# Attention by pairs of heads: scores as three 64-row matmuls in two row halves

## The chip, the cores and the metric

The kernel runs on one core of a Trainium2 chip. The time is the device time of one execution in microseconds; the median of three runs is given. Engines are named as in the profile: PE is TensorE (matmul), PEld its weight load, DVE is VectorE, ACT is ScalarE, POOL is GpSimd, SP is the engine whose queue issues the DMAs. L12 is line 12 of the kernel.

## The reference

One layer of a decoder trunk on 2048 positions of 1024 channels: a projection of the normalised input feeds three groups (an mLSTM of 4 heads, forgetting attention of 8 heads of 64, a spatial gating unit); their outputs go through `w_out`, then follows a convolutional FFN. The change concerns the attention:

```python
F = jnp.cumsum(jax.nn.log_sigmoid(f_pre), axis=-1)
for blk in range(s_len // Q_BLOCK):                  # blocks of 128 queries
    lo, hi = blk * Q_BLOCK, (blk + 1) * Q_BLOCK
    logits = (jnp.einsum('bhtd,bhsd->bhts', q[:, :, lo:hi], k[:, :, :hi]) * scale
              + F[:, :, lo:hi, None] - F[:, :, None, :hi])
    logits = jnp.where(mask, logits, -jnp.inf)       # causal
    p = jax.nn.softmax(logits, axis=-1)
    outs.append(jnp.einsum('bhts,bhsd->bhtd', p, v[:, :, :hi]))
```

q and k are RMS-normalised per head first. All is float32; the kernel's large matmuls run on float32r and split each operand in a rounded part (hi) and a remainder (lo), so that a product takes several matmuls.

## The kernel before

The stages in order of time: a projection by blocks of 256 columns of `w_in` (with the mLSTM in the background), attention, the `w_out` product, the FFN up and down. Tiles come from pools with tags; each tag has a fixed number of buffers, and a tile waits for the last user of its buffer. A scheduler orders the instructions of each engine when the program is built, so that steps of neighbouring loops stand between each other; the source gives the dependences and a priority.

*Projection of q and k* (`use_qk`, `turn`). For each of 16 row tiles of 128 positions and each group of four heads, L639 scales the projected columns by the norm and writes each head twice side by side (`[P, 4, 2, 64]`), four transposes (L648) turn it, ACT writes the hi part (L653 for q, L659 for k) and DVE the lo part (L655, L660). q goes to DRAM as two tensors, `qh_d` and `ql_d`, each with a head's 64 channels twice on 128 partitions; k as one, `kk_d`, with hi on partitions 0 to 63 and lo on 64 to 127.

*Scores* (`scores(h, tb)`), for head `h` and block `tb` of 512 queries. For each of four row blocks of 128 queries the keys up to the diagonal are walked in pieces of 512. A piece takes a PSUM tile `sp` (four buffers of 2 KB a partition) and two matmuls on all 128 rows, hi q by [k hi; k lo] (L190) and lo q by the same (L191), which gives all four products; on the last piece a bfloat16 matmul adds the causal mask (L193). One DVE operation adds the forget bias and takes the row maximum of the piece (L198, which comes with a read of the accumulator). Then follow the maximum over pieces (L203), the exponential with its sum on ACT (L206, pieces of 1024), the reciprocal of the sum (L209 to L212) and the scaling on POOL (L214).

*Values* (`finish(h, tb)`). For each of the 4 to 16 key blocks `j`, up to four transposes of 128x128 (L227) go to PSUM tile `tp` (three buffers), ACT takes the hi part (L230), DVE the lo part (L231), and two matmuls (L232, L233) add to `op` (one buffer). V holds hi and lo side by side, so that partitions 0 to 63 and 64 to 127 of `op` are summed at the end (L235, L236) and stored.

The loop runs over 8 heads and 4 blocks, `scores` and then `finish` of the same block. K, the bias row and V of a head are loaded whole (`load_head`). The last head takes the blocks in the order 2, 3, 0, 1, in which `w_out` uses them. The first half of `w_out` is loaded and split (`load_w`, L130, L131) after block 2 of head 6.

*Elsewhere 64-row matmuls occur* in the mLSTM (`mlstm`, L804 and L806), where two heads lie on the two halves of the partitions:

```python
for par in range(2):
    hp = slice(par * 64, par * 64 + 64)
    eo = mps()
    for j in range(2):
        T.matmul(eo[:, j * P : (j + 1) * P], kT[hp, j, :], qT[hp, j, ch], start=True, stop=True)
    for j in range(2):
        T.matmul(eo[:, 256 + j * 65 : 321 + j * 65], qT[hp, j, ch], Cst[hp, j, :], start=True, stop=True)
```

These operands are float32, for which the trace has two matmuls for each.

## Time and profile before

| | |
|---|---|
| median of three runs | 2768.22 us (2767.72 to 2775.49) |
| profiled execution | 2769.87 us, span 2768.2 us, granted clock 0.978 |
| PE busy | 2638.0 us, 95% |
| PEld busy | 2247.4 us, 81% |
| DVE busy | 2089.8 us, 75% |
| ACT busy | 1314.6 us, 47% |
| POOL busy | 374.6 us, 14% |

The span runs from the first to the last instruction. A group row reads: line, engine, operation, output<-inputs, shapes, count, busy us, mean ns of one, idle time of the engine before them and what ended it. [...] A timeline row reads: start, us, engine, line, operation, tiles, shape, count; a shape `64*128` says that 64 rows and 128 columns of the array are used.

### The profile page before, as it was taken

How to read it: one execution, taken by the hardware profiler on the slowest of the kernel's cores; microseconds unless marked ns; L12 is line 12 of the kernel's file. 1: busy time of each engine (PE TensorE's matmuls, PEld its weight loads, DVE VectorE, ACT ScalarE, POOL GpSimd, SP SyncE). 2: the span in 40 equal slices, each digit the busy share in tenths (PEclk: the TensorE clock that was granted, in tenths of full speed). 3: DMA queues.
4: the chain of work that ended last, by engine and by line, in shares of the span. 5: the costliest groups of instructions: out<-in, count | busy, mean ns of one | idle time of the engine just before them, and what ended most of it. 6: DMA issues, size and time to landing. Idle time of an engine off the chain costs nothing.

```text
span 2768.2 us, 40628 instructions
## 1 busy us (share of the span) xinstructions
PE 2638.0 (95%) x14473; PEld 2247.4 (81%) x14473; DVE 2089.8 (75%) x4090; ACT 1314.6 (47%) x2448; POOL 374.6 (14%) x400
## 2 busy tenths in 40 slices
PE   5989899989899999999998999999999999999999
PEld 5989888989797877767886888888788888888787
DVE  7366477246448999997567988887888887899797
ACT  4243244233226788776444544444444444444443
POOL 2032221032223334342000000000000000000000
PEclk9989999999899999999999999999999999999999
DMA  7534375324446234323663222227322223848533
GB/s 247 175 93 144 112 229 176 108 48 134 111 145 197 79 108 132 106 79 130 218 242 91 93 76 84 84 76 281 99 84 78 82 84 141 303 146 297 185 106 115
DMA packets 322561, 382.11 MB, mean 138 GB/s; under 512 B 28189, under 2 KB 227833, under 8 KB 320309
## 3 DMA queue, kind: packets, MB, share of 16 engines
q1 hardware_dynamic: 322356, 379.51, 42.3%
q8 instruction: 114, 1.87, 0.3%
q14 instruction: 91, 0.74, 0.1%
HBM read 274.47 MB, written 104.96 MB: 137 GB/s over the span
## 4 chain that ended last, share of the span: by engine, by line
PE 61%; DVE 5%; ACT 2%; issue 1%; DMA 1%; POOL 0%; DVEq 0%; ACTq 0%; POOLq 0%
PE ub L54 10%; PE ub L55 10%; PE ub L56 10%; PE db L55 4%; PE db L56 4%; PE db L54 4%; PE tp L227 4%; PE op L232 2%; PE op L233 2%; PE wps L56 2%; PE wps L54 2%; PE wps L55 2%; PE sp L190 2%; PE sp L191 1%; ACT L L206 1%
## 5 line engine op out<-in xcount | busy, mean ns | idle before, releaser
L54 PE MATMUL acc<-whi,hh 128*128 128x256 f32 (+1 forms) x1408 | 423.0, 301 | 23.8 <-DVE qn L639 10.5
L56 PE MATMUL acc<-whi,hl 128*128 128x256 f32 (+1 forms) x1408 | 411.1, 293 | 0.9 <-DVE hl L487 0.9
L55 PE MATMUL acc<-wlo,hh 128*128 128x256 f32 (+1 forms) x1408 | 411.3, 293 | 0.0
L54 PEld LDWEIGHTS acc<-whi,hh 128*128 128x128 f32 x1408 | 281.9, 200 | 30.9 <-DVE vhl L625 5.4
L55 PEld LDWEIGHTS acc<-wlo,hh 128*128 128x128 f32 x1408 | 282.3, 201 | 0.5 <-issue 0.2
L56 PEld LDWEIGHTS acc<-whi,hl 128*128 128x128 f32 x1408 | 281.3, 200 | 1.6 <-DVE hl L487 1.4
L54 PE MATMUL ub<-T,wsph 128*128 128x512 f32 x704 | 276.2, 393 | 5.8 <-ACT wsph L1150 5.8
L55 PE MATMUL ub<-T,wsph 128*128 128x512 f32 x704 | 276.0, 392 | 0.0
L56 PE MATMUL ub<-T,wspl 128*128 128x512 f32 x704 | 274.9, 391 | 0.4 <-DVE wspl L1151 0.4
L55 PE MATMUL db<-wspl,wsph 128*128 128x512 f32 x616 | 240.3, 390 | 1.9 <-DVE wspl L1282 1.9
L56 PE MATMUL db<-wsph,wspl 128*128 128x512 f32 x616 | 239.6, 389 | 0.0
L54 PE MATMUL db<-wsph 128*128 128x512 f32 x616 | 238.2, 389 | 0.3 <-ACT wsph L1281 0.3
L1150 ACT CAST wsph<-S 128x512 fp32r<-128x512 f32 x176 | 109.4, 621 | 231.4 <-PE ub L55 166.6
L56 PE MATMUL ub<-B,wspl 128*128 128x512 f32 x528 | 208.2, 394 | 2.1 <-DVE wspl L1151 2.1
L54 PE MATMUL ub<-B,wsph 128*128 128x512 f32 x528 | 208.4, 395 | 1.5 <-ACT wsph L1150 1.5
L55 PE MATMUL ub<-B,wsph 128*128 128x512 f32 x528 | 208.0, 394 | 0.0
L214 POOL TENSOR_SCALAR L<-L,ri 128x1024 f32<-128x1024 f32 (+2 forms) x192 | 168.3, 890 | 260.5 <-DVE nm L203 69.5
L206 ACT ACTIVATE L<-L,nm 128x1024 f32<-128x1024 f32 (+2 forms) x192 | 173.2, 903 | 55.7 <-DVE nm L203 54.5
L231 DVE TENSOR_TENSOR plo<-tp,phi 128x512 fp32r<-128x512 f32 (+1 forms) x320 | 186.8, 607 | 16.9 <-ACT phi L230 11.2
L198 DVE CUSTOM_DVE_ANT_0 L<-sp,nfb 128x512 f32<-128x512 f32 (+2 forms) x320 | 185.4, 601 | 5.5 <-PE sp L191 1.9
L227 PE MATMUL tp<-ident,L 128*128 128x128 f32 x1088 | 178.4, 276 | 6.1 <-POOL L L214 2.9
L230 ACT CAST phi<-tp 128x512 fp32r<-128x512 f32 (+1 forms) x320 | 157.7, 519 | 32.1 <-PE tp L227 28.3
(336 smaller groups left out, 6040.5 us busy)
## 6 DMA issues: line engine op xcount, KB each, us to landing
w<-in_w_up_dram SPq DMA_DIRECT2D x88, 512.0 KB
wd<-in_w_down_dram SPq DMA_DIRECT2D x176, 256.0 KB
wa<-in_w_ada_dram SPq DMA_DIRECT2D x96, 256.0 KB
wst<-in_w_in_dram SPq DMA_DIRECT2D x48, 512.0 KB
act_d<-yc SPq DMA_DIRECT2D x44, 512.0 KB
act<-act_d SPq DMA_DIRECT2D x44, 512.0 KB
hc_d<-hl SPq DMA_DIRECT2D x28, 512.0 KB
xt<-in_x_dram SPq DMA_DIRECT2D x16, 512.0 KB
```

Of the source, the lines that this page charges most:

```text
L54: T.matmul(ps, lh, rh, start=start, stop=False, skip_group_check=resume)
L55: T.matmul(ps, lh, rl, start=False, stop=False, skip_group_check=resume)
L56: T.matmul(ps, ll, rh, start=False, stop=stop, skip_group_check=resume)
L190: T.matmul(sp[:, :w], q2[0][:, qs], kk[:, s0 : s0 + w], start=True, stop=False)
L198: V.tensor_tensor_reduce(out=parts[-1][0][:, o : o + w], in0=sp[:, :w], in1=nf[:, s0 : s0 + w], scale=1.0, scalar=-3.0e38, op0=ALU.add, op ...
L206: A.activation(L[:, :w], L[:, :w], AF.Exp, bias=nm, accum_out=rs[:, j : j + 1])
L214: G.tensor_scalar(L[:, :w], L[:, :w], ri, 1.0, op0=ALU.mult, op1=ALU.mult)
L227: T.transpose(tp[:, i * P : (i + 1) * P], rows[i][j // 8][:, (j % 8) * P : (j % 8 + 1) * P], ident)
L230: A.copy(hi[:, c0:], tp[:, c0:])
L231: V.tensor_tensor(lo[:, c0:], tp[:, c0:], hi[:, c0:].bitcast(F32), op=ALU.subtract)
L232: T.matmul(op[:, c0:], vv[:, j, :], hi[:, c0:], start=(j == 0), stop=False)
L1150: A.copy(hi, src)
```

## The change

Heads are taken in four pairs. Head `2p` has partitions 0 to 63 and head `2p + 1` partitions 64 to 127 of every q and k tile.

- In the projection, `turn` no longer doubles a head's channels: L639's successor writes 256 columns for 512, two transposes for four turn a tile, and q and k each are stored as a hi and a lo tensor (`q_d`, `k_d`) of half the former size per tensor.
- `scores(p, tb)` is a generator. It walks the keys in chunks of up to 1024 for both heads at once, each head with its own PSUM tile `sp` (two buffers of 4 KB a partition). The mask is added first. Each 512 columns take three matmuls a head on its 64 rows (hi hi, hi lo, lo hi), written so that the two heads alternate. The DVE operation covers the chunk, keeps a running minimum of the negated logits across chunks (its start value is the first chunk's), and a separate maximum is not taken. The sum of two chunks is on POOL for both heads at once, one reciprocal serves both heads. Exponentials of the second head, reciprocal and scaling of a row block are held back behind the next DVE operations (`after`).
- `finish(p, tb, rows)` is a generator over both heads; its value products stand two steps behind the transposes (`behind`). `tp` and `op` have two buffers each.
- `phase(now, then)` steps the scores of block `now` and the values of the block before, `then`, in turn.
- The first block (pair 0, block 1) is written between the steps of the last projection block (`background`, `tick`).
- K and bias are loaded a pair ahead, V in four chunks; `w_out`'s first half is loaded at the last block of pair 3.

```diff
-    qh_d = dr.tile([NH, P, S], F32, name="qh_d")
-    ql_d = dr.tile([NH, P, S], F32, name="ql_d")
-    kk_d = dr.tile([NH, P, S], F32, name="kk_d")
+    q_d = dr.tile([NH // 2, 2, P, S], F32, name="q_d")
+    k_d = dr.tile([NH // 2, 2, P, S], F32, name="k_d")
...
-        pp.open("att_r", "right", ("sp", 2048, 4))
+        pp.open("att_r", "right", ("sp", 4096, 2))
...
-        pp.open("att_l", "left", ("tp", 2048, 3), ("op", 2048, 1))
+        pp.open("att_l", "left", ("tp", 2048, 2), ("op", 2048, 2))
...
+    def scores(p, tb, q2, rows):
+        kh, kl, nf = kv["k", p]
+        qh, ql = q2
+        after = []
         for i in range(4):
             n_s = (tb * 4 + i + 1) * P
-            npc = (n_s + 511) // 512
+            parts = [(s0, min(1024, n_s - s0)) for s0 in range(0, n_s, 1024)]
...
-                sp = pp.tile([P, 512], F32, name="sp")
-                last = j == npc - 1
-                T.matmul(sp[:, :w], q2[0][:, qs], kk[:, s0 : s0 + w], start=True, stop=False)
-                T.matmul(sp[:, :w], q2[1][:, qs], kk[:, s0 : s0 + w], start=False, stop=not last)
+                sp = [pp.tile([P, 1024], F32, name="sp", tag="sp") for _ in range(2)]
+                last = c == len(parts) - 1
                 if last:
-                    T.matmul(sp[:, w - P : w], identb, maskb, start=False, stop=True)
+                    for e in range(2):
+                        T.matmul(sp[e][:, w - P : w], identb, maskb, start=True, stop=False, skip_group_check=True)
+                for b in range(0, w, 512):
+                    bw = min(512, w - b)
+                    for n, (q_, k_) in enumerate(((qh, kh), (qh, kl), (ql, kh))):
+                        for e in range(2):
+                            hp = slice(e * 64, e * 64 + 64)
+                            T.matmul(
+                                sp[e][:, b : b + bw], q_[hp, qs], k_[hp, s0 + b : s0 + b + bw],
+                                start=n == 0 and not (last and b + bw == w), stop=n == 2, skip_group_check=True,
+                            )
+                for e in range(2):
+                    L[e, c] = pool.tile([P, w], F32, name="L", tag=l_tag(p, tb, i, e, c))
+                    V.tensor_tensor_reduce(
+                        out=L[e, c], in0=sp[e][:, :w], in1=nf[:, e, s0 : s0 + w], scale=-1.0,
+                        scalar=3.0e38 if c == 0 else nm[:, 2 * e : 2 * e + 1], op0=ALU.add, op1=ALU.min,
+                        accum_out=nm[:, 2 * e + c : 2 * e + c + 1],
+                    )
+                    if after:
+                        after.pop(0)()
+                    yield
...
+            def second(exps=exps, rs=rs, rr=rr, n=len(parts)):
+                exps(1)
+                if n == 2:
+                    G.tensor_tensor(rs[:, 0:2], rs[:, 0:2], rs[:, 2:4], op=ALU.add)
+
+            def third(L=L, rs=rs, rr=rr, n=len(parts)):
+                V.reciprocal(rr, rs[:, 0:2])
+                for e in range(2):
+                    for c in range(n):
+                        G.tensor_scalar(L[e, c], L[e, c], rr[:, e : e + 1], 1.0, op0=ALU.mult, op1=ALU.mult)
+
+            exps(0)
+            after += [second, third]
...
+        for e in range(2):
+            op = pp.tile([P, 512], F32, name="op", tag="op")
+            for j in range(ns):
...
+                behind.append((e, j, c0, hi, lo, op))
+                if len(behind) > 2:
+                    product(*behind.pop(0))
+                yield
...
+    def phase(now, then):
...
+        for n in range(n_sc):
+            next(sc)
+            while done < (n + 1) * (n_fin - 6) // n_sc:
+                next(fin)
+                done += 1
...
-            n = pool.tile([P, 4, 2, 64], F32, name="qn", tag="q2k")
+            n = pool.tile([P, 4, 64], F32, name="qn", tag="q2k")
...
-            for j in range(4):
-                T.transpose(tp[:, j * P : (j + 1) * P], n[:, j].rearrange("p e d -> p (e d)"), ident)
+            for j in range(2):
+                T.transpose(tp[:, j * P : (j + 1) * P], n[:, 2 * j : 2 * j + 2].rearrange("p e d -> p (e d)"), ident)
...
+    for p in range(4):
+        for n, tb in enumerate((1, 2, 3, 0) if p < 3 else TBS):
+            if n == 0:
+                if p < 3:
+                    load_k(p + 1)
+                load_v(p, 0)
+                load_v(p, 1)
+            if (p, n) == (3, 3):
+                pool.close("att_r")
+                wout_open_right()
                 load_w(0)
+            last = phase((p, tb), last) if (p, n) != (0, 0) else (0, 1, first_rows)
```

## The prediction

> **What bounds the kernel now.** I read the page's engine shares, then busy time by stretch to find the stage that the change touches, then the groups by line there, then the timeline for what one instruction really occupies.

> ```profile
> span 2768.2 us, 40628 instructions
> PE 2638.0 (95%) x14473; PEld 2247.4 (81%) x14473; DVE 2089.8 (75%) x4090; ACT 1314.6 (47%) x2448; POOL 374.6 (14%) x400
> 830.00:1290.00 460.00, 443.29 (x2614) 347.33 (x2613) 421.56 (x1344) 354.06 (x763) 177.45 (x200) 0.99 0.37 112
> 880.00:1200.00 320.00, 313.04 (x1878) 248.84 (x1876) 302.00 (x980) 257.02 (x561) 130.70 (x148) 1.00 0.36 111
> 947.60:1158.10 210.50, 206.77 (x1249) 165.38 (x1249) 198.97 (x660) 168.62 (x371) 83.15 (x98) 1.00 0.35 112
> ```

> In the stretches the columns are PE, PEld, DVE, ACT and POOL busy time, granted clock, DMA share and GB/s. Attention is 830 to 1290 us, the other stages hold no changed loop but the projection's q and k blocks. 947.6 to 1158.1 is four heads: 52.6 us a head, TensorE idle for 0.9 of them and VectorE for 2.9. Both are near full; ACT (42 a head) and DMA (0.35) are not.

> A busy PE is not a PE at its peak, so I take what a matmul occupies from start to start:

> ```profile
> 860.25 0.40 PE L191 MATMUL sp<-kk,q 128*128 128x512 f32 x1
> 860.48 0.39 PE L190 MATMUL sp<-kk,q 128*128 128x512 f32 x1
> 860.71 0.39 PE L233 MATMUL op<-plo,vv 128*128 128x512 f32 x1
> 861.75 0.92 PE L227 MATMUL tp<-ident,L 128*128 128x128 f32 x7
> ...
> 865.12 0.23 PE L193 MATMUL sp<-maskb,identb 128*128 128x128 bf16 x1
> ...
> 865.16 0.47 PE L190 MATMUL sp<-kk,q 128*128 128x512 f32 x1
> ```

> 512 columns cost 0.23 us; a transpose (0.92 - 0.27)/6 = 0.109, a mask 0.04. Per head the causal blocks are 136 squares of 128: 17,408 columns. Two score matmuls over them are 68 x 0.23 = 15.6 us, two value matmuls the same, 136 transposes 14.8, masks under 1: 46.7 of the 52.6. The other 5.9 a head (47 for eight) is idleness and weight loads that stand open after a wait.

> **The scores on TensorE.** Before, one head's hi and lo halves fill all 128 rows: 2 matmuls a piece, 640 in all, 278,528 columns, 544 x 0.23 = 125 us. After, 3 matmuls a piece on 64 rows for each head of a pair: 960, 417,792 columns. They gain only where the two row halves run side by side. The kernel already has 64-row matmuls, in the mLSTM part:

> ```profile
> 772.10 0.28 PE L55 MATMUL acc<-wlo,hh 128*128 128x256 f32 x1
> 772.22 0.28 PE L56 MATMUL acc<-whi,hl 128*128 128x256 f32 x1
> 772.43 0.71 PE L804 MATMUL mps<-qT,kT 64*128 64x128 f32 x4
> 772.98 0.22 PE L806 MATMUL mps<-Cst,qT 64*128 64x65 f32 x1
> 772.98 0.37 PE L804 MATMUL mps<-qT,kT 64*128 64x128 f32 x1
> 773.03 0.38 PE L806 MATMUL mps<-Cst,qT 64*128 64x65 f32 x2
> 773.20 0.27 PE L804 MATMUL mps<-qT,kT 64*128 64x128 f32 x1
> 773.26 0.27 PE L806 MATMUL mps<-Cst,qT 64*128 64x65 f32 x1
> 773.31 0.38 PE L804 MATMUL mps<-qT,kT 64*128 64x128 f32 x2
> 773.53 0.55 PE L806 MATMUL mps<-Cst,qT 64*128 64x65 f32 x4
> 774.01 0.44 PE L648 MATMUL trp<-ident,qn 128*128 128x128 f32 x2
> ```

> Two things stand there. First, the L804 of the second half (from 772.98) start between the L806 of the first, though the program has all of the first half's ahead of them: six starts in 0.4 us, 0.06 each against 0.11 alone. So the halves do run side by side, and from some matmuls apart. [...]

> Second, a change between 128 and 64 rows costs. Into it: 772.22 to 772.43 is 0.21 where 0.12 is usual (+0.09), and the four L804 take 0.71 where 0.27 + 3 x 0.11 = 0.60 would do (+0.10). Out of it: the last L806 starts at 773.81 and the transposes at 774.01, 0.20 where 0.11 is usual (+0.09), and their pair takes 0.44 for 0.38 (+0.06). A round trip is 0.34 us. [...]

> What decides is how often the built program changes mode, since its order on TensorE isn't that of the source: the scheduler moves steps between each other. A stretch of it (line, tiles, shape, count):

> ```
> L259 Matmult op<-phi,vc 128x512
> L210 Matmult sp<-k,q 128x128
> L275 Matmult tp<-ident,L 128x128 x4
> L260 Matmult op<-plo,vc 128x512
> L275 Matmult tp<-ident,L 128x128 x4
> L259 Matmult op<-phi,vc 128x512
> L260 Matmult op<-plo,vc 128x512
> L259 Matmult op<-phi,vc 128x512
> L210 Matmult sp<-k,q 128x128
> ```

> The 960 score matmuls (L210) stand in 222 groups between 128-row work; 66 groups are a single matmul, 145 hold one half only, and the 128-row masks cut further ones. If within a group the shorter half hides wholly beside the longer, 304,000 columns remain: 594 x 0.23 = 137 us, +12 against 125. (All pairs side by side would be 208,896, 94 us, -31; none 417,792, 188 us, +63. I take +12, as the rows show overlap inside such a group and none can cross 128-row work.) The 222 round trips at 0.34 are 75 us; 184 of the groups begin with no wait of their own, and I take these: +63. [...]

> **VectorE and the waits.** Rows of what goes or shrinks:

> ```profile
> L198 DVE CUSTOM_DVE_ANT_0 L<-sp,nfb 128x512 f32<-128x512 f32 x224 | 150.3, 682 | 5.5 <-PE sp L191 1.9 <-PE sp L193 1.8 <-PE tp L227 1.7
> L198 DVE DVE_READ_ACCUMULATOR2_ANT mx<- 128x1 f32 x320 | 26.4, 82 | 0.0
> L203 DVE TENSOR_REDUCE nm<-mx 128x1 f32<-128x4 f32 (+3 forms) x95 | 13.2, 145 | 0.4 <-DVE ri L212 0.2
> L209 DVE TENSOR_TENSOR ri<-rs 128x1 f32<-128x1 f32 x64 | 14.0, 219 | 1.4 <-POOL L L214 0.5 <-ACT L L206 0.4
> L212 DVE RECIPROCAL ri<-rs 128x1 f32<-128x1 f32 x64 | 10.1, 158 | 5.2 <-ACT L L206 3.5
> L198 DVE CUSTOM_DVE_ANT_0 L<-sp,nfb 128x256 f32<-128x256 f32 x32 | 13.3, 415 | 0.0
> PEld sp L190 <- DVE mx L198: 13.2, 30, 1.5
> PEld op L233 <- DVE plo L231: 13.2, 42, 1.1
> L127 POOL TENSOR_TENSOR ss<-ss,nhalf 128x4 f32<-128x4 f32 x64 | 69.5, 1087 | 203.6 <-DVE ss L636 196.9 <-DVE st L440 6.7
> ```

> Pieces of 512 become pieces of 1024: 192 for 320. (682 - 415)/256 is 1.04 ns a column, so 150 ns of a piece are fixed: 128 x 0.15 = 19 us, and 128 reads of the accumulator, 10. The 128 row maxima (0.145) go, 19; 64 sums move to POOL, 32 of two columns, 14 off VectorE; 64 of 128 reciprocals go, 10. That is 72 us off VectorE, 9 of its 50 a head. With TensorE now longer, VectorE isn't what ends attention, so this is worth only the waits of TensorE on it: of the 47 us above I take 20 (the two waits quoted are 26), ends 0 and 47. On POOL the 32 sums are about 1.1 us each (as its other small operation) beside 460 us of which it is busy 177: nothing; without that cover 35. ACT's exponentials and copies keep their columns: nothing. The new write of products two steps behind, and one step of scores per few steps of values, is what the scheduler already does across blocks (score, value and transpose rows alternate at 860 us): nothing, at most the 7 us of idleness that TensorE has in 320 us. [...]

> **The projection.** A k or q tile now takes 2 transposes for 4:

> ```profile
> L648 PE MATMUL trp<-ident,qn 128*128 128x128 f32 x256 | 38.8, 280 | 4.8 <-DVE qlo L655 3.4 <-DVE qhi L660 1.2 <-DVE ss L636 0.3
> L639 DVE TENSOR_TENSOR qn<-acc,ss 128x512 f32<-128x512 f32 x64 | 43.8, 690 | 38.8 <-POOL ss L127 35.8 <-PE trp L648 2.4
> PE acc L54 <- DVE qn L639: 10.5, 12, 3.4
> 640.00:700.00 60.00, 56.98 (x470) 55.36 (x470) 42.52 (x85) 18.78 (x33) 13.13 (x9) 1.00 0.46 135
> kk_d<-qhi SPq DMA_DIRECT2D x32, 256.0 KB
> qh_d<-qhi SPq DMA_DIRECT2D x32, 256.0 KB
> ql_d<-qlo SPq DMA_DIRECT2D x32, 256.0 KB
> ```

> 128 x 0.109 = 14 us on an engine that is full there (57 of 60): -14. The halved scaling (690 to about 415 ns, by the 256-column row) can shorten the 10.5 us of waits: end -25. The stores halve for q, and for k are two of 128 KB for one of 256: 32 more issues on SP, and a k tile takes two of the three staging buffers, so that ACT may wait for a landing as q does today; end 0. I take -14.

> **The end.** The w_out block is loaded and split at the last block of pair 3, not a head earlier: 16 loads of 256 KB through three buffers in some 25 us of remaining attention, before the y loads on the same queue. At 112 GB/s as in attention, 4 MB would be 37 us, at the 232 GB/s of the stretch after 1292 18 us. 0 to +12; I take 0, since the queue has little else then.

> ```profile
> 1292.00:1400.00 108.00, 107.97 (x509) 89.87 (x508) 63.57 (x109) 46.40 (x92) 10.35 (x13) 1.00 0.65 232
> ```

> **Sum.** +12 (score stream) + 63 (mode changes) - 20 (waits on VectorE) - 14 (projection) = +41. The profiled execution took 2769.9 us (span 2768.2), 1.7 above the median of 2768.2: 2811, to be measured as about 2810.

> **Rivals.**
> [...] Chance 0.25.
> Nothing to measure: 0.10 to 0.17 us a group, within 8 us (0.3%, about what a measurement can tell). Chance 0.08.
> [...] Chance 0.12.
> Forecast, 0.17 to 0.40 us a group: 2785 to 2830. Chance 0.55.

> **How the numbers follow.** Faster 0.25, same 0.08, slower 0.67. The forecast's own range is 2785 to 2830; with the faster rival's likelier half and most of the serial rival, 2745 to 2860 leaves out about 2 in 10.

> **What would show it.** Right: attention over 500 us with TensorE busy near 97% and VectorE under 80%; score matmuls 0.2 us late after a transpose or value product and transposes 0.1 to 0.2 late after them; two L210 of unlike halves starting within 0.05 us inside groups; the projection 10 to 20 us earlier at its end. Wrong: transposes following L210 at 0.23 us, or attention under 450. If L210 starts are 0.23 apart throughout, the pairing has failed. If TensorE idles on `ld` after attention, the end term was mine to have kept.

## The result and the profile after

The changed kernel takes 2894.95 us (median of four runs, 2890.11 to 2907.38); the kernel before took 2769.68 beside it. The ratio is 1.0456 (95% interval 1.0425 to 1.0487): slower by some 125 us, where the prediction had 41 and a range that ended at 2860. The profiled execution of after is its slowest run, 2907.38 us, 137.5 over the profiled one of before; its granted clock over the whole program is 0.959 and that of the other three 0.964 to 0.966, which by that difference is worth some 15 us.

The page of after, engine shares and two rows of the 40 slices (tenths; PEclk is the granted clock):

```profile
PE 2751.0 (95%) x14665; PEld 2284.4 (79%) x14665; DVE 2033.6 (70%) x3578; ACT 1311.5 (45%) x2448; POOL 379.1 (13%) x432
PE   6989799998979999999999899999999999999999
PEclk9989899999989979789999999999999999999999
```

TensorE is as busy as before by its share of the span. In attention (slices 12 to 20) the clock row falls to 7 or 8 in four slices. The stage's ends come from the timeline: the projection's last transpose starts at 848.0 before and at 836.3 after, attention's last value product at 1290.1 and 1425.5. So the projection gained 11.7 us, attention went from 442 to 589 us, and what follows is unchanged (1478 and 1480 us). Busy time by stretch, first the whole attention before:

```profile
848.00:1290.10 442.10, 427.19 (x2494) 333.09 (x2492) 408.99 (x1305) 346.22 (x745) 171.72 (x193) 0.99 0.36 110
```

and after, the whole, its first 20 us and five stretches of 50:

```profile
836.30:1425.50 589.20, 552.55 (x2782) 383.80 (x2781) 384.11 (x793) 352.32 (x737) 167.53 (x220) 0.88 0.20 66
840.00:860.00 20.00, 7.38 (x26) 5.75 (x26) 3.58 (x6) 2.35 (x5) 0.00 (x0) 0.59 1.00 368
950.00:1000.00 50.00, 49.85 (x278) 35.54 (x278) 36.79 (x76) 31.97 (x67) 9.29 (x12) 1.00 0.24 76
1000.00:1050.00 50.00, 48.76 (x216) 32.86 (x215) 30.20 (x62) 27.89 (x60) 15.94 (x22) 0.73 0.06 16
1050.00:1100.00 50.00, 47.58 (x195) 31.51 (x194) 25.80 (x62) 25.53 (x57) 17.27 (x23) 0.73 0.25 90
1150.00:1200.00 50.00, 48.61 (x210) 32.84 (x210) 31.06 (x66) 26.58 (x58) 17.35 (x24) 0.73 0.06 16
1200.00:1250.00 50.00, 47.55 (x199) 31.46 (x198) 26.79 (x62) 27.70 (x61) 17.38 (x24) 0.73 0.10 27
```

The column after POOL is the granted clock. Before it is 0.99 over attention, after 0.88: 0.12 x 589 = 71 us of clock are missing, 4 before. The stretches at 0.73 get through a quarter fewer matmuls (195 to 216 for 280) although TensorE is "busy" 47.5 us of 50 and more. In the trace the clock is a half for 136 us of attention: four blocks of 27.3 us (from 1011, 1069, 1165 and 1223), 24 us in shorter ones before 896 and one of 3.4 at 1400.

The start has a wait of its own. The chain of waits and SP's timeline:

```profile
841.84 14.14 DMA vc<-v_d
```

```profile
840.15 0.44 SPq L160 DMA_DIRECT2D k<-k_d  x1
840.68 0.59 SPq L161 DMA_DIRECT2D k<-k_d  x1
841.37 0.38 SPq L162 DMA_DIRECT2D nf<-nf_d  x1
841.84 10.48 SPq L167 DMA_DIRECT2D vc<-v_d  x4
```

The next pair's K and bias row (4 MB) are issued ahead of the first V chunk, which lands 14 us later; TensorE works 7.4 of the 20 us.

What one instruction occupies, from the timeline at full clock:

```profile
911.71 0.28 PE L260 MATMUL op<-plo,vc 128*128 128x256 f32 x1
911.92 2.78 PE L210 MATMUL sp<-k,q 64*128 64x512 f32 x12
914.63 0.66 PE L275 MATMUL tp<-ident,L 128*128 128x128 f32 x4
...
960.95 0.40 PE L259 MATMUL op<-phi,vc 128*128 128x512 f32 x1
961.27 0.38 PE L210 MATMUL sp<-k,q 64*128 64x256 f32 x1
961.59 0.66 PE L275 MATMUL tp<-ident,L 128*128 128x128 f32 x4
962.00 0.48 PE L260 MATMUL op<-plo,vc 128*128 128x512 f32 x1
962.32 0.60 PE L275 MATMUL tp<-ident,L 128*128 128x128 f32 x4
962.67 0.48 PE L259 MATMUL op<-phi,vc 128*128 128x512 f32 x1
```

Two readings. From 960.95 the product is followed after 0.32 (0.23 usual), the score matmul of 256 columns after 0.32 (0.12 usual), and the four transposes take 0.41 until the next product starts, where the next four (from 962.32), without a change of mode ahead of them, take 0.35: together 0.09 + 0.20 + 0.06 = 0.35 us for a change of mode and back, where the prediction read 0.34 at 772 us. And the twelve score matmuls from 911.92 take 2.71 us: twelve one after another would take 12 x 0.23 = 2.76, in two streams of six side by side 1.38. In TensorE's order as the program was built, this group is six matmuls of one half and then six of the other; another is shown beside it:

```
911.92  AAAAAABBBBBB   (A, B: the row half of each of the 12 score matmuls)
904.92  BABABABAB      9 matmuls in 1.36 us
```

The starts show an overlap only where the halves meet or alternate. So a mixed group isn't yet a group side by side.

### The profile page after: what moved, and what is told of

It is laid out like the page before. It is cut to its first block, busy times and chain, and to the rows that moved or that the text cites. A ratio compares the mean times of both kernels' runs of the same rounds, so it can differ in the third digit from the quotient of the medians.

```text
span 2905.7 us, 40534 instructions
## 1 busy us (share of the span) xinstructions
PE 2751.0 (95%) x14665; PEld 2284.4 (79%) x14665; DVE 2033.6 (70%) x3578; ACT 1311.5 (45%) x2448; POOL 379.1 (13%) x432
## 4 chain that ended last, share of the span: by engine, by line
PE 62%; DVE 6%; DMA 2%; ACT 1%; issue 1%; POOL 0%; SPq 0%; DVEq 0%; ACTq 0%; POOLq 0%
PE ub L56 10%; PE ub L54 10%; PE ub L55 10%; PE sp L210 6%; PE tp L275 5%; PE db L55 3%; PE db L56 3%; PE db L54 3%; PE op L260 2%; PE op L259 2%; PE wps L55 2%; PE wps L56 2%; PE wps L54 2%; DVE wspl L1355 1%; DMA wd<-in_w_down_dram 1%
## 5 line engine op out<-in xcount | busy, mean ns | idle before, releaser
L54 PE MATMUL acc<-whi,hh 128*128 128x256 f32 (+1 forms) x1408 | 423.1, 301 | 22.3 <-DVE qn L708 11.2
L56 PE MATMUL acc<-whi,hl 128*128 128x256 f32 (+1 forms) x1408 | 411.3, 293 | 0.0
L55 PE MATMUL acc<-wlo,hh 128*128 128x256 f32 (+1 forms) x1408 | 411.3, 293 | 0.0
L54 PEld LDWEIGHTS acc<-whi,hh 128*128 128x128 f32 x1408 | 282.2, 201 | 29.4 <-ACT qhi L718 7.4
L55 PEld LDWEIGHTS acc<-wlo,hh 128*128 128x128 f32 x1408 | 282.5, 201 | 0.4 <-issue 0.2
L56 PEld LDWEIGHTS acc<-whi,hl 128*128 128x128 f32 x1408 | 281.2, 200 | 0.9 <-DVE hl L556 0.6
L54 PE MATMUL ub<-T,wsph 128*128 128x512 f32 x704 | 276.2, 393 | 5.8 <-ACT wsph L1223 5.8
L56 PE MATMUL ub<-T,wspl 128*128 128x512 f32 x704 | 274.8, 391 | 1.4 <-DVE wspl L1224 1.4
L55 PE MATMUL ub<-T,wsph 128*128 128x512 f32 x704 | 276.1, 392 | 0.0
L278 ACT CAST phi<-tp 128x512 fp32r<-128x512 f32 (+1 forms) x320 | 164.1, 519 | 176.1 <-PE tp L275 155.2
L55 PE MATMUL db<-wspl,wsph 128*128 128x512 f32 x616 | 240.3, 390 | 2.3 <-DVE wspl L1355 2.3
L56 PE MATMUL db<-wsph,wspl 128*128 128x512 f32 x616 | 239.6, 389 | 0.0
L54 PE MATMUL db<-wsph 128*128 128x512 f32 x616 | 238.3, 389 | 0.3 <-ACT wsph L1354 0.3
L210 PE MATMUL sp<-k,q 64*128 64x512 f32 (+3 forms) x960 | 234.0, 422 | 0.5 <-DVE nm L216 0.3
L54 PE MATMUL ub<-B,wsph 128*128 128x512 f32 x528 | 208.5, 395 | 2.8 <-ACT wsph L1223 2.8
L56 PE MATMUL ub<-B,wspl 128*128 128x512 f32 x528 | 208.4, 395 | 0.7 <-DVE wspl L1224 0.7
L275 PE MATMUL tp<-ident,L 128*128 128x128 f32 x1088 | 198.9, 302 | 10.4 <-DVE plo L279 8.9
L55 PE MATMUL ub<-B,wsph 128*128 128x512 f32 x528 | 208.1, 394 | 0.0
L210 PEld LDWEIGHTS sp<-k,q 64*128 64x128 f32 x960 | 138.9, 200 | 67.1 <-issue 39.2
L275 PEld LDWEIGHTS tp<-ident,L 128*128 128x128 f32 x1088 | 134.3, 151 | 72.8 <-DVE plo L279 28.1
## 6 DMA issues: line engine op xcount, KB each, us to landing
wd<-in_w_down_dram SPq DMA_DIRECT2D x176, 256.0 KB
wa<-in_w_ada_dram SPq DMA_DIRECT2D x96, 256.0 KB
```

Of the source, the lines that this page charges most:

```text
L54: T.matmul(ps, lh, rh, start=start, stop=False, skip_group_check=resume)
L55: T.matmul(ps, lh, rl, start=False, stop=False, skip_group_check=resume)
L56: T.matmul(ps, ll, rh, start=False, stop=stop, skip_group_check=resume)
L210: T.matmul(sp[e][:, b : b + bw], q_[hp, qs], k_[hp, s0 + b : s0 + b + bw], start=n == 0 and not (last and b + bw == w), stop=n == 2, skip_ ...
L275: T.transpose(tp[:, i * P : (i + 1) * P], rows[e][i][j // 8][:, (j % 8) * P : (j % 8 + 1) * P], ident)
L278: A.copy(hi[:, c0:], tp[:, c0:])
```

## A ledger of attention

The runs below are read against this sum, each by its one profiled execution. A term is the excess over the attention of before (442.1 us). Scores: columns side by side, as in the prediction, x 0.45 ns, less 125. Pairing missed: what the groups with both halves took at full clock above that, with their 0.19 us of mode change inside taken off; it is 1.26 times the ideal in after, and 25 us in each kernel when scaled to all groups. Mode: groups x 0.35. Clock: (1 - granted clock of the stretch) x length, less 4. Rest: what is left, with all waits and whatever the other terms have wrong; it makes each row close by construction.

| kernel | excess | scores | pairing missed | mode (groups) | clock | rest |
|---|---|---|---|---|---|---|
| after | +147 | +12 | +25 | +78 (222) | +66 | -34 |
| V first | +118 | +13 | +24 | +78 (224) | +29 | -26 |
| three transpose buffers | +75 | +4 | +25 | +61 (173) | +16 | -31 |
| pair tile | +96 | -31 | +25 | +51 (147) | +23 | +28 |
| all mended | +62 | -30 | +26 | +49 (141) | +11 | +6 |
| scores on 128 rows | +94 | +63 | 0 | 0 | +12 | +19 |

The clock is rounded to 0.01, so its term is good to 3 us. With the terms that come from the order and the clock, the first three kernels are told apart to within 8 us. That rest is negative, as the prediction had it (-20), isn't borne out by TensorE's waits: by the rows of 900 to 1280 us it waits 43 us for other engines in after and 49 before, and in all of attention it is idle for 37 us (12 of them the wait for V) and 15. So part of the 0.35 for each group may be too much. With the 184 groups that the prediction counted, the mode term is 64 and rest is -20, and the first three rows agree as well. The ledger can't tell these two apart; 66 and 25 us, of the clock and of the missed pairing, stand in both.

## The experiments

**V chunks ahead of the next pair's K.**

```diff
-                if p < 3:
-                    load_k(p + 1)
                 load_v(p, 0)
                 load_v(p, 1)
+                if p < 3:
+                    load_k(p + 1)
```

> Edit: the V chunks of a pair are loaded ahead of the next pair's K and bias instead of behind them. Theory A: the 14.1 us in which the first value product waits for vc (841.8 to 856.1 us in the profile of the changed kernel) is the price of that order on the one DMA queue; the time falls by 10 to 14 us, to about 2882, and the rest of attention stays as it is. Rival: the transfers only trade places and the next pair's K comes late instead; no change within 0.3%.

Measured: 2887.22 us, ratio 1.0399 (1.0384 to 1.0415), 16 us better than after by the ratios. The V wait is gone from the start, but the next block's q, now behind K and the bias, is late instead. Chain of waits, then two stretches:

```profile
850.64 16.36 DMA q<-q_d
867.04 1.90 PE sp L210 x12
```

```profile
840.00:860.00 20.00, 12.71 (x55) 9.71 (x54) 6.75 (x13) 5.76 (x12) 1.84 (x2) 0.66 0.80 287
870.00:915.00 45.00, 42.56 (x129) 27.28 (x129) 20.32 (x48) 20.10 (x44) 13.87 (x21) 0.51 0.15 46
```

The half clock moved as well: one block of 44 us right behind the stall, and hardly any later. By the ledger the run's gain is the clock's (71 us missing became 34; each is of one execution), and little is left for the V wait itself. So the order of loads costs, but what it costs is mixed with where the clock falls.

**Scores on all 128 rows.** The structure of the change without 64-row matmuls: q of each head lies on its half and zeros, written by POOL, on the other.

```diff
+                G.memset(t[op_].bitcast(F32), 0.0)
...
-                            hp = slice(e * 64, e * 64 + 64)
...
-                                sp[e][:, b : b + bw], q_[hp, qs], k_[hp, s0 + b : s0 + b + bw],
+                                sp[e][:, b : b + bw], q_[e][:, qs], k_[:, s0 + b : s0 + b + bw],
```

> Edit: the changed kernel with its score matmuls on all 128 rows: q of each head is loaded into a tile whose other half is zero, so 960 matmuls of 128 rows and no 64-row group in attention (three buffers fewer elsewhere to make room). Theory A (mode changes cost 0.35 us each, and the thin stream that they leave makes the clock fall to a half): score stream 188 us for 137 (+51), 222 changes of mode gone (-78), the 110 us at half clock in attention gone (-55): 2895 - 82 = about 2813, granted clock 1.0 throughout attention. Rival B (the loss lies in the new structure: tiles of 1024, two buffers, the phases, work held back): the waits stay, the stream grows: 2895 + 51 = about 2945, with half-clock stretches as now.

Measured: 2865.19 us, ratio 1.0321 (1.0305 to 1.0336): 37 us faster than after by the ratios, and some 50 slower than the theory. The clock did as the theory said; the time did not. Two stretches:

```profile
851.00:871.00 20.00, 6.01 (x26) 4.70 (x27) 3.66 (x7) 2.61 (x5) 2.41 (x5) 0.51 0.88 318
1000.00:1050.00 50.00, 48.67 (x277) 39.09 (x276) 39.31 (x86) 35.30 (x79) 21.97 (x31) 1.00 0.12 33
```

From 950 us to 1350 the granted clock is 1.00 in every stretch of 50 us, with the same loops, the same order of loads and the same tiles in PSUM. Three passes on all rows beat the three in two halves here. Against before the sum closes to 5 us (ledger, last row): the score stream, half as long again, is 63 us, the start's stall, in this run too, 14, and the low clock that goes with it (0.51 there) 12, of 94. So by this run the rest of the new structure costs little.

Against after the sum does not close, and the start's stall isn't the reason, as it stands in the 2895 too. By the ledger the pairing that was missed goes as well, which the theory left out, and rest climbs from -34 to +19. Some 12 of these 53 us are the experiment's own: TensorE waits for POOL's zeros (7.4 and 5.1 us in 900 to 1280). The others are waits that return with the shorter stream, or charges to the 64-row groups that are too high; this run doesn't tell which. The projection also ended at 851.3 us for 836.3, for a reason not followed.

**Mode changes in the kernel before.** A 64-row matmul of 128 columns on zeros ahead of each mask, 128 of them; it adds zero.

```diff
                 if last:
+                    T.matmul(sp[:, w - P : w], zb[0:64], maskb[0:64], start=False, stop=False)
                     T.matmul(sp[:, w - P : w], identb, maskb, start=False, stop=True)
```

> Edit: the kernel before, with one more matmul per row block of scores: 64 rows, zero weights, 128 columns, added to the last piece ahead of the mask (128 in all). It measures a change of mode by itself. Theory A: 128 x (0.35 + 0.06) = 52 us if TensorE is the bound, half of that if waits that stand there absorb some: +26 to +52, 2796 to 2822; the clock stays at 1.0 in attention. Rival: changes of mode fall into waits: at most +8, 2770 to 2778.

Measured: 2792.96 us, ratio 1.0066 (1.0049 to 1.0083), 18 us: 0.14 us a group, between the rival and the theory. From start to start the trace has 0.255 a group (0.097 into it, 0.158 to the mask), so nearly half of it was absorbed. The next run asks whether that is the price or slack used up.

**More of them, where TensorE waits for little.** The same matmul between the two value products, 320 times.

```diff
             T.matmul(op[:, c0:], vv[:, j, :], hi[:, c0:], start=(j == 0), stop=False)
+            T.matmul(op[:, c0 : c0 + P], zb[0:64], maskb[0:64], start=False, stop=False)
             T.matmul(op[:, c0:], vv[:, j, :], lo[:, c0:], start=False, stop=(j == ns - 1))
```

> The kernel before with a 64-row matmul of 128 columns on zeros between the two value products of each block of 128 tokens: 320 more changes of mode, none in the scores. It adds zero, so what is computed stays. In the run with 128 of them a group took 0.255 us more from start to start and 0.14 in the total time. Theory (the other half fell into waits, and these are used up): 320 x 0.255 = 82 less at most 20, so 2835 to 2865. Rival (0.14 us is what a change costs in this stream, so that the 222 of the changed kernel account for 30 us only): 2775 + 45, so 2815 to 2825.

Measured: 2857.65 us, ratio 1.031 (1.0294 to 1.0326), 86 us: 0.27 a group, at the upper end of the theory. Timeline:

```profile
1000.84 0.28 PE L234 MATMUL op<-phi,vv 128*128 128x256 f32 x1
1001.05 0.23 PE L235 MATMUL op<-maskb,zb 64*128 64x128 bf16 x1
1001.21 0.39 PE L236 MATMUL op<-plo,vv 128*128 128x256 f32 x1
```

0.21 and 0.16 stand there for 0.12 and 0. So slack absorbed part of the 128 (0.14 us paid of 0.255), and each of the 320 cost its full price (0.27). The granted clock is 1.00 from 900 to 1260 us and 0.99 over attention, as before: these changes of mode alone did not lower it.

**A tile for both heads, matmuls kept together.** `sp` holds 512 columns of both heads (two buffers), and the score matmuls have priority in the scheduler: 147 groups, nearly all with both halves alternating.

```diff
-                sp = [pp.tile([P, 1024], F32, name="sp", tag="sp") for _ in range(2)]
...
+                    sp = pp.tile([P, 2, 512], F32, name="sp", tag="sp")
...
+                    with tc.high_priority():
...    (in it the masks and the six score matmuls of 512 columns)
```

> Edit: the changed kernel with the scores of both heads in one PSUM tile of 2 x 512 columns (two buffers), and their matmuls at a higher priority for the scheduler, so that the halves stand together: 147 groups of 64-row matmuls for 222, and 205,400 columns for 304,000 when the shorter half hides beside the longer. Pieces are 512 wide again on VectorE. Theory A: score stream 92 us for 137 (-45), 75 changes of mode fewer (-26), and less or no time at half clock (0 to -55): 2770 to 2825. Rival B: the structure is what costs: within 10 us of 2895 or above, as VectorE gets 128 operations more.

Measured: 2863.26 us, ratio 1.0315 (1.0299 to 1.033): between the two expectations, 39 us better than after by the ratios. By the ledger the shorter score stream gives 43 us, the fewer groups 27 and the clock 43, and new waits take back 62, which leaves 51 in attention of the two profiled executions. Waits in 900 to 1280 us:

```profile
PEld tp L279 <- DVE plo L283: 39.3, 85, 0.9
PEld op L263 <- ACT phi L282: 23.6, 26, 2.5
DVE rr L246 <- POOL rs L243: 19.5, 17, 4.0
PEld sp L213 <- DVE nm L219: 18.6, 42, 1.0
PE tp L279 <- DVE plo L283: 12.0, 35, 0.7
```

**All of it mended.** The pair tile with V ahead of K, three transpose buffers and one output buffer, and the sum of a row's two parts on VectorE.

```diff
-        pp.open("att_l", "left", ("tp", 2048, 2), ("op", 2048, 2))
+        pp.open("att_l", "left", ("tp", 2048, 3), ("op", 2048, 1))
...
-                    G.tensor_tensor(rs[:, 0:2], rs[:, 0:2], rs[:, 2:4], op=ALU.add)
+                    V.tensor_tensor(rs[:, 0:2], rs[:, 0:2], rs[:, 2:4], op=ALU.add)
```

> This is the changed kernel with the score tiles of a pair in one 2-bank buffer and the score matmuls kept together (as in the run with the pair tile), and with three more things put as they were before: the V loads ahead of the next pair's K, three transpose buffers and one output buffer, and the two parts of a row's sum added on VectorE and not on POOL. Theory (what the mode changes and the clock leave over is structure: the late V, TensorE waiting 51 us for VectorE's low halves through two transpose buffers, VectorE waiting 20 us for POOL's sum): 16 + about 40 + about 15 off the pair-tile run, 2863 less 60 to 75, so 2785 to 2805, and the wait of the transposes on the low halves falls under 15 us. Rival (the bursts of exponentials and the 147 changes of mode are the cost, and the other waits only move): 2835 or more, with the removed waits turning up at another place.

Measured: 2832.85 us, ratio 1.021 (1.019 to 1.0229). It gains 30 us of the 60 to 75 that the theory had, and ends 2 us from the rival's figure. By the ledger 22 of them are waits and 12 the clock. The wait on the low halves fell from 51 to 26 us, not under 15; the wait for a read score tile stayed. Waits in 900 to 1280 us:

```profile
PEld sp L213 <- DVE nm L219: 19.0, 48, 1.0
PEld tp L279 <- DVE plo L283: 14.3, 9, 3.2
PE tp L279 <- DVE plo L283: 12.2, 7, 3.0
```

A group in its timeline shows what the change can do at its best:

```profile
936.41 0.42 PE L263 MATMUL op<-phi,vc 128*128 128x384 f32 x1
936.75 0.96 PE L213 MATMUL sp<-k,q 64*128 64x512 f32 x6
937.65 0.44 PE L264 MATMUL op<-plo,vc 128*128 128x384 f32 x1
```

Six matmuls of 512 columns in 0.90 us, 3 x 0.23 and 0.19 of the change of mode. The kernel before takes 4 x 0.23 = 0.92 for the same two heads and no change. Side by side the three matmuls save at most 31 us in all (208,896 columns for 278,528, at 0.45 ns each), and 141 changes at 0.35 cost 49. At that price this form loses with tiles of 512 columns even when everything pairs.

**Three transpose buffers and one output buffer alone.** Only the buffer line of the run above, on the changed kernel.

> The changed kernel with three buffers for the transposes and one for the value products, as before, and nothing else. The scheduler also answers to it: its order has 173 groups of 64-row matmuls for 222. Theory (two transpose buffers hold TensorE back, and thin the stream until the clock drops): 15 to 50 us off, 2845 to 2880, and less half clock. Rival (the buffers don't matter, since two products are kept behind): 2885 to 2905 but for 49 changes of mode at 0.14 to 0.34 us, 7 to 17 us, so 2870 or more.

Measured: 2844.71 us, ratio 1.0249 (1.0234 to 1.0265), 57 us better by the ratios. One line of buffers gives more than any other single edit. It isn't by the waits of TensorE on them (20 us in after, 15 here): the scheduler answers with 173 groups for 222 (-17 at 0.35), and the clock holds better. The stretch:

```profile
842.00:1359.10 517.10, 486.86 (x2779) 363.31 (x2778) 383.91 (x793) 346.80 (x737) 169.21 (x220) 0.96 0.24 76
```

0.04 x 517 = 21 us of clock are missing for 71, -50. Together -67; the two profiled spans differ by 65. Why the clock holds better with this order isn't shown.

**The sum on VectorE alone.** Only the `tensor_tensor` line of the mended kernel.

> The changed kernel with the 32 sums of two columns on VectorE and not on POOL, and nothing else. Theory (the reciprocal on VectorE waits for POOL, whose sum stands behind some 4.5 us of scaling, and with it the whole queue of VectorE): the 14 us of that wait go, 5 to 15 us off, 2880 to 2890. Rival (VectorE has slack there): within 5 us of 2895.

Measured: 2909.56 us, ratio 1.049 (1.0433 to 1.0546): not better, a miss for the theory; the interval has after's ratio in it. Its granted clock in attention is 0.88 as in after. Its four runs go from 2897 us at a clock of 0.965 over the whole program to 2932 at 0.948: the same kernel, with the time following the clock.

**VectorE's part alone, on the kernel before.** Score tiles of 1024 columns in two buffers, one reduction for two, a running minimum.

```diff
-        pp.open("att_r", "right", ("sp", 2048, 4))
+        pp.open("att_r", "right", ("sp", 4096, 2))
...
-                    scalar=-3.0e38, op0=ALU.add, op1=ALU.max, accum_out=mx[:, j : j + 1],
+                    scalar=3.0e38 if c == 0 else nm[:, 0:1], op0=ALU.add, op1=ALU.min, accum_out=nm[:, c : c + 1],
```

> The kernel before with the VectorE part of the change alone: score tiles of 1024 columns in two buffers, one reduce per tile with a running minimum, no separate row maximum. Scores stay on all 128 rows. Some 58 us come off VectorE. Theory (VectorE's relief is worth part of TensorE's waits, the coarser tiles cost nothing): 2745 to 2765. Rival (the coarser tiles make TensorE wait for a whole tile to be read, which is part of the structure's price): 2776 or more, with waits of the score matmuls on VectorE above the 13 us that they are before.

Measured: 2791.39 us, ratio 1.0058 (1.0041 to 1.0075): the rival. Waits in 900 to 1280 us:

```profile
PEld sp L193 <- DVE nm L198: 20.7, 36, 1.2
PE sp L193 <- DVE nm L198: 12.0, 24, 1.0
DVE L L198 <- PE sp L194: 11.5, 23, 2.3
```

TensorE and VectorE now wait for each other at the score tiles (44 us by three rows); VectorE in attention went only from 409 to 398 us. Relief that comes with coarser tiles is worth less than nothing here.

**Two transpose and two output buffers alone, on the kernel before.**

```diff
-        pp.open("att_l", "left", ("tp", 2048, 3), ("op", 2048, 1))
+        pp.open("att_l", "left", ("tp", 2048, 2), ("op", 2048, 2))
```

> The kernel before with two transpose buffers and two output buffers, for three and one, and nothing else. Theory (with VectorE at 94% two buffers make TensorE wait for the low halves, as the 51 us of the pair-tile run): 15 to 45 us more, 2785 to 2815. Rival (the buffers cost nothing by themselves, and what three buffers gave the changed kernel came through the clock and the order alone): within 5 us of 2772.

Measured: 2830.07 us, ratio 1.0195 (1.018 to 1.021), 54 us, above the theory's range. Waits in 900 to 1280 us:

```profile
PEld op L232 <- ACT phi L230: 40.7, 120, 1.2
PEld op L233 <- DVE plo L231: 30.0, 72, 0.9
```

Before has 6.8 and 11.7 us of these two. There the source has the value product right behind its transposes, and without the third buffer TensorE waits for the copies. The changed kernel holds products back by two steps and has 6 us of the first wait, which would fit its `behind` hiding in after what the buffers cost in before; no run takes `behind` away.

**Score matmuls as one block.** V first, three transpose buffers, and the matmuls of a tile in a critical block (`with tc.tile_critical():` around them): 95 groups, all but 6 with both halves.

> The changed kernel with the score matmuls of a tile held together as one block in TensorE's order, the V loads ahead of the next pair's K, and three transpose buffers for two. The order then has 95 groups of 64-row matmuls for 222, all but 6 with both halves, 205,400 columns side by side for 304,000. Ledger theory (against before: the score stream, 0.35 us for each group, half of the time at half clock, and waits by themselves): -33 + 33 + 5 to 15 for the clock, and some 20 to 50 of waits, since a block now stands until both tiles are read: 2800 to 2840. Rival (the changes of mode are nearly all of the loss): within 15 us of before, 2765 to 2790.

Measured: 3073.3 us, ratio 1.1088 (1.1066 to 1.1109), far from both expectations. Waits, and the stretch they are from:

```profile
DVE L L217 <- PEq L201: 113.6, 33, 6.9
PEld sp L205 <- issue: 70.0, 32, 4.5
```

```profile
900.00:1260.00 360.00, 250.23 (x1358) 179.02 (x1358) 180.89 (x383) 169.16 (x357) 83.50 (x111) 0.80 0.16 53
```

The block makes TensorE stand until all is ready and holds VectorE up behind it: TensorE is idle for 110 of 360 us and the clock is 0.80. It tells nothing of fewer changes of mode, but shows again a thin TensorE stream and a low clock together.

**A filler.** A 128-row matmul of zeros as wide as the product, between the two value products of the changed kernel, at every second block of 128 tokens (160) or at every one (320).

```diff
             T.matmul(op[:, c0:], v, hi[:, c0:], start=(j == 0), stop=False)
+            if j % 2:
+                T.matmul(op[:, c0:], zb[:, 0:P], zb[:, c0:], start=False, stop=False)
             T.matmul(op[:, c0:], v, lo[:, c0:], start=False, stop=(j == ns - 1))
```

> The changed kernel with a 128-row matmul of zeros (bf16, as wide as the product) between the two value products of every second block of 128 tokens: 160 of them, about 66,000 columns or 30 us of TensorE's stream that do nothing but fill it; what is computed stays. The order has 202 groups of 64-row matmuls for 222, worth 7 us less. Theory (the half clock comes of a thin stream): half clock in attention falls from 136 us to under 60, so 30 - 7 - 40 or more: 2895 goes to 2860 to 2885, though work is added. Rival (the clock drops for another reason of this kernel, its 64-row work or its waits): half clock stays above 110 us, and 2895 + 23 = 2910 to 2925.

> The same filler at every block of 128 tokens: 320 matmuls, 139,000 columns, 62 us; the order has 180 groups, 15 us less. Theory (thin stream): half clock under 30 us in attention, 53 to 60 us of lost time gone: 2895 + 62 - 15 - 55 = about 2887, 2870 to 2900. Rival (another reason): 2930 to 2950 with the half clock above 110 us.

Measured: 2899.09 us (ratio 1.0444, 1.0429 to 1.046) and 2907.36 us (1.0475, 1.0457 to 1.0492). Attention's stretch of the first and of the second:

```profile
839.90:1413.80 573.90, 543.53 (x2939) 377.73 (x2938) 385.25 (x793) 349.83 (x737) 168.50 (x220) 0.92 0.21 68
```

```profile
840.60:1422.30 581.70, 554.26 (x3095) 385.46 (x3094) 386.03 (x793) 350.56 (x737) 168.15 (x220) 0.94 0.21 67
```

The granted clock rises with the filler, 0.88, 0.92, 0.94, and the half clock falls from 136 us to 89 and 65, so the direction is the theory's; but it was to fall below 60 and 30, and both times lie between the bands of the theory and of the rival. 30 and 62 us of added stream moved the time by -3 and +5 us by the ratios; the fewer groups pay 7 and 15 of that, and the clock (71 us missing, then 46 and 35) most of the rest. So a fuller stream went with a higher clock, and filling it is no remedy. Since the filler also moves the scheduler's order, how much of the clock it bought by itself stays open, and with it whether the thin stream is the cause.

**The projection alone.** Two transposes and 256 columns a tile, stores by pairs, before's attention with two loads for one.

```diff
...    (the loads of q; the projection as in the change)
-            dma(t.bitcast(F32), d[h, :, tb * TB : (tb + 1) * TB])
+            for n in range(2):
+                dma(t[n * 64 : n * 64 + 64].bitcast(F32), q_d[h // 2, d, e : e + 64, tb * TB : (tb + 1) * TB])
```

> The projection's part of the change alone: two transposes and 256 columns a k or q tile for four and 512, hi and lo parts stored by pairs of heads; the attention is that of before, whose loads put each head's rows on both halves with two DMAs for one. Theory (TensorE is full there, and attention starts earlier by what it saves): 10 to 14 us off, 2760 to 2767. Rival (the stores and the doubled loads, on one queue, give it back): within 4 us of 2775.

Measured: 2757.04 us, ratio 0.9947 (0.9934 to 0.9959): 15 us faster than before, a little more than the theory had, and the fastest kernel here. Attention's stretch:

```profile
835.80:1276.70 440.90, 425.72 (x2495) 331.02 (x2493) 408.89 (x1311) 347.23 (x749) 172.49 (x195) 1.00 0.39 109
```

The projection ends at 835.8 for 848.0, and attention takes what it took, though the loads are twice as many.

**The projection and a running minimum.** As above, and in before's scores the separate row maximum replaced by a running minimum, tiles kept at 512 columns.

> The run with the projection alone, and in the attention of before the running minimum in place of the separate row maximum: score tiles stay 512 wide in four buffers, and 128 reductions (0.145 us each on average, 13 us for the 95 of the commonest shape) go from VectorE. Theory (VectorE at 94% in attention holds TensorE back by part of its 47 us): 3 to 10 us better than the projection alone, 2752 to 2763. Rival (each reduce now waits for the one before it, as they already stand in one queue: no gain): within 3 us of the projection alone.

Measured: 2767.57 us, ratio 0.9984 (0.9976 to 0.9993): 10 us worse than the projection alone, a miss for both. Groups by line:

```profile
L201 DVE CUSTOM_DVE_ANT_0 L<-sp,nfb,mx 128x512 f32<-128x512 f32 x120 | 89.5, 746 | 4.6 <-PE sp L194 1.8
L201 DVE CUSTOM_DVE_ANT_0 L<-sp,nfb 128x512 f32<-128x512 f32 x104 | 70.7, 681 | 2.5 <-PE sp L194 1.3 <-PE tp L229 1.1
```

A reduction that starts from the last one's result takes 65 ns more than one that starts from a constant; at that price the 192 of them are some 12 us, about as much as the reductions that went. That would explain why nothing is gained, not why 10 us are lost: attention is 452 us for 441, with TensorE's waits spread over five rows, and the cause was not followed further.

## Why the prediction was wrong

Its direction and its reason stand: changes of mode on TensorE outweigh what pairing saves. Its size fell short by some 85 us. The step that failed is the sum's silence on the clock, and beside it the columns taken as side by side. In attention the sum had 12 + 63 - 20 = +55; the profiled execution has +147 there (+135 at attention's end). The 92 between are 66 of the clock and 25 of pairing missed. Step by step:

- *No term for the clock.* This is the largest miss, 66 us in the profiled execution and, with the other runs' higher clock, an estimated 50 in the median one. The prediction costed every instruction at the clock of before (0.99 to 1.00 in its rows) and never asked whether the change would lower it; it fell to 0.88.
- *"If within a group the shorter half hides wholly beside the longer, 304,000 columns remain."* It doesn't. In TensorE's order the nine from 904.92 alternate and take 1.36 us, where one after another would be 2.07; the built order also has groups that hold all of one half and then all of the other, as the twelve from 911.92 (2.71 us). By the ledger that is 25 us that the +12 lacked. The rows at 772 us showed an overlap of short matmuls near to each other, and I carried it to groups of any order.
- *"184 of the groups begin with no wait of their own, and I take these: +63."* The price of 0.34 us stood where it was read again (0.35 at 961 us). How many of the 222 were paid isn't settled: the 320 added changes took 0.27 each of 0.255, the 128 of the smaller run 0.14, so where TensorE has no slack each is paid in full. With all 222 the term is +78 and the next one -34; with 184 they are as predicted.
- *"of the 47 us above I take 20".* The rest of the ledger is -34, or -20 with the prediction's own count of changes, in both cases with the V stall in it. The waits by the trace fell by 6 us only, so where the gain lies isn't shown.
- *V loads behind the next pair's K* were not in the sum. The stall is 12 us of TensorE idle in after; putting V first brought 16 us, by the ledger mostly through the clock.
- *The projection, -14.* 11.7 in after, 15 alone: right, and it needs no pairs of heads in attention.
- *The end at nothing.* Right: what follows attention took 1478 us before and 1480 after.
- *The new structure at nothing.* No price for it shows in after or in the run on 128 rows, but that is partly luck: on the kernel before two transpose buffers cost 54 us and the wide score tiles 15, which after seems to hide with products held back and a VectorE with slack. It fails as soon as the scores are grouped (the pair tile, rest +28).
- *VectorE, 72 us less.* The whole program has 56 less, of which 17 are the projection's scaling (64 operations of 422 ns for 690); so attention has some 39 of the 72.
- *What would show it:* attention over 500 us, VectorE under 80%, unlike halves starting together inside groups, transposes 0.1 to 0.2 late behind the scores: so it was (589 us, 65%, 0.20). The score matmuls came 0.09 late, not 0.2. TensorE was to be near 97% busy in attention and was at 94%; at half clock that share says little.
- *Ends of the rivals.* With all 222 groups, 0.17 us each gives 38 and, with the other terms (12 - 20 - 14 = -22), +16 and not "within 8 us", and 0.40 gives 2837 and not 2830. It changes nothing here, as the measured time lies beyond both.

The serial rival (the halves one after the other) and the forecast were both partly true, and neither had the clock.

## What to carry to other kernels

Before 64-row matmuls are set side by side, count the changes of mode in the order as built: at the 0.35 us each that this trace has, a group must save more than that, and what it saves hung here on the order (nine with the halves alternating took 1.36 us, six and then six 2.71). Three passes side by side for the four of two heads save one pass, 0.45 ns a column, so here a group must cover some 780 score columns of both heads to pay for its 0.35 us. The pair tile sets 512 side by side, and the block of up to 1024 lost more by its waits. And when a change thins TensorE's stream, ask what the granted clock will do: look at its column in the stretches first, as the busy share did not show it here (0.73 with TensorE busy for 47.5 us of 50). A change of several parts may hold a good one: the projection's two transposes for four were worth 15 us by themselves.
